# A hybrid decoder trunk in fp32 on one core: three norms without GpSimd, ten early pairs instead of seven, results ahead of other steps

## The chip, the cores and the metric

The kernel runs on one core of a Trainium2 chip. The metric is device time in microseconds of one execution; lower is better. The core has a matrix engine (PE in the profile), VectorE (DVE), ScalarE (ACT), GpSimd (POOL) and SyncE (SP), which here only starts DMAs. Each engine works through its own queue strictly in the order in which the instructions stand there, and waits for the others by semaphores. Matmul results lie in PSUM and are taken out by DVE or ACT.

## The reference

Two layers over a sequence of 1024 tokens with 1024 channels. Each layer has a token mixer and a SwiGLU FFN, both behind an RMS norm that is scaled and shifted by the conditioning.

```python
for l in range(DEPTH):
    mod = (c_act @ ada_w[l] + ada_b[l])[:, None, :]
    sh_m, sc_m, gt_m, sh_f, sc_f, gt_f = jnp.split(mod, 6, axis=-1)
    h = rms_norm(x, norm_mix[l]) * (1 + sc_m) + sh_m
    ...
        y = hybrid_mixer(h, ...)
    ...
        y = retention_mixer(h, ret_w_in[i], ret_w_out[i])
    x = x + gt_m * y
    h = rms_norm(x, norm_ffn[l]) * (1 + sc_f) + sh_f
    x = x + gt_f * swiglu(h, ffn_w_in[l], ffn_w_out[l])
```

`swiglu` is `(silu(g) * u) @ w_out` with `g, u` the halves of `h @ w_in` (2816 channels each). The retention's input product gives queries and keys, values and gates.

## The kernel before

**Layout and precision.** Activations lie transposed, channels on the 128 partitions: x is eight tiles x0 to x7 of 128 x 1024 tokens, and most work is done on a half of 512 tokens. Each fp32 operand v is split into a rounded part hi (a cast on ACT) and a remainder lo = v - hi (a subtraction on DVE or POOL), and a product takes three matmuls: hi hi, lo hi, hi lo (`mm3`, L161 to L163). Weights come by DMA as `raw` (512 KB), `w_split` makes `whi` (L141, ACT) and `wlo` (L142, DVE).

**Three large products with a norm ahead of them**: the FFN of layer 0, the retention's input product, the FFN of layer 1. Each stands behind an out product (`out_gen`) that runs one token half after the other; an output tile's eviction (L309, DVE) adds it to x. Two PSUM tiles take turns there, so that a group of 12 matmuls waits for the eviction two groups earlier. When the first half of x is done, `norm_ops` makes the norm of that half while the out product's second half still runs; the second half's norm follows.

**The norm.** `norm_stat` (L188) squares the eight tiles on ACT and adds them up: POOL takes five of the seven additions, DVE the two last. A matmul with a constant matrix (`nps`, L201) sums over the channels, `rsqrt` (L170 to L177) makes the root on ACT and DVE. `value` (L1210, L1211) makes a normed tile, `parts` (L1214, L1215) its hi and lo; every second lo of A11, A12 and A22 is on POOL, and a string ENGS says which engine makes the rest.

**The product.** The three products (of the retention all but the values) use a Strassen-Winograd scheme with seven block products instead of eight. A11, A12 are the first token half (upper and lower channels), A21, A22 the second; S1 to S4 are sums of these (L1251 to L1254, four steps each), split again into hi and lo (128 x 1024 each, `split`). B11 to B22 are blocks of a pair of weight tiles, T1 to T4 sums of them, made and split in `prep_b` (L1320 to L1328). `wino` runs over pairs. For a pair n: m1 multiplies A11 B11 and copies the result to u2 (L1350, ACT); m2 adds A12 B21 in the same PSUM bank, after that copy; m67 takes S2 T2 and S3 T3 (L1382, L1384), m5 S1 T1 (c22, L1391), m4 A22 T4, m3 S4 B22 in the bank of m5, after c22's addition has read it, and end (L1402) finishes u3. A block product has 12 matmuls (L1338 to L1340).

**Early pairs.** Only m1 and m2 need the first token half alone. In the FFNs they run ahead for the first NE = 7 pairs (`early`), with their results u2 and sg spilled to DRAM (`spill`) and read back in the main loop (`reload`); the weights of such a pair are loaded twice. sg has one buffer. Pair n's m2 follows its m1; the second half's norm is carried on after m1 of pair 1. The retention has no early pairs: its values (`v_rows`, L1771, evacuated by L1774 on ACT into two stage tiles) are multiplied on the first half meanwhile, three heads of four weight tiles each.

**What sets the order.** A scheduler places instructions of all engines by their dependences, its own estimates of duration, and a priority that `tc.high_priority(offset=...)` raises. The evictions L309 and the norm have 3000.

Of the kernel before, what the change touches and what calls it, by code (L numbers as in the profile page):

```python
# [13 lines left out]
ALU = mybir.AluOpType  # L14
# [4 lines left out]
D = 1024  # L19
# [14 lines left out]
GW = {'X': 1.4, 'W': 1.0, 'Y': 1.4, 'r': 1.0, 'v': 1.0, 'S': 1.2}  # L34
GSTAG = 14
EVP = 3000
NE = 7
ENGS = 'VGVGGGVVGGVGVVV'
EBS = 'VVVVVVVVV'
ECS = 'VVVVVVVGVVVVVVVVV'  # L40
RC = (2, 4)
# [21 lines left out]
def tile_trunk(ctx: ExitStack, tc: tile.TileContext, xT, cT, adaS, adaT, vec, w_ab, w_hyb, w_hout, w_rin, w_rout,  # L63
# [123 lines left out]
    def norm_stat(xs, scr, half):  # L187

        sl = slice(half * HT, half * HT + HT)
        acc = scr(1)  # L190
        for k in range(8):
            if k == 0:
                A.activation(acc, xs[k][:, sl], AF.Square)
            else:
                sq = scr(2 + k % 2)
                A.activation(sq, xs[k][:, sl], AF.Square)
                (V if k > 5 else G).tensor_tensor(acc, acc, sq, op=ALU.add)

        def rest():
            ps = pst.tile([P, HT], F32, tag="st", name="nps")  # L200
            PE.matmul(ps, onesD, acc, start=True, stop=True)  # L201
            y = scr(0)
            rsqrt(ps, y, acc)
            return y
        return rest
# [988 lines left out]
    def norm_ops(o, xs, pool, ni, kept, a21=None):  # L1194

        l, f = ni // 2, ni % 2
        half = int(bool(kept))
        sl = slice(half * HT, half * HT + HT)
        ts = {}

        def scr(i):
            if i == 0:
                return pool.tile([P, HT], F32, tag="ny", name="ny")
            j, r = divmod(i - 1, 2)
            if j not in ts:
                ts[j] = slot(12 + j, F32, "nscr")
            return ts[j][:, r * HT:r * HT + HT]

        def value(k, y, dst):
            V.scalar_tensor_tensor(dst, xs[k][:, sl], modA[:, ni * 8 + k:ni * 8 + k + 1], y, op0=ALU.mult, op1=ALU.mult)  # L1210
            A.activation(dst, dst, AF.Identity, bias=mcol(l, 3 * f, k))  # L1211

        def parts(hi, lo, v, eng):
            A.copy(hi, v)  # L1214
            eng.tensor_tensor(lo, v, hi.bitcast(F32), op=ALU.subtract)  # L1215

        part = lambda v, k: v[k // 2][:, (k % 2) * HT:(k % 2) * HT + HT]
        with tc.high_priority(offset=3000):
            rest = norm_stat(xs, scr, half)
        yield  # L1220
        with tc.high_priority(offset=3000):
            y = rest()
        if half == 0:
            kept["S3"] = [slot(14 + j, F32, "h11") for j in range(2)]
            kept["S4"] = [slot(22 + j, F32, "h12") for j in range(2)]
            for j in range(8):
                k, nm, v = j % 4, ("A11", "A12")[j // 4], part(kept[("S3", "S4")[j // 4]], j % 4)
                value(j, y, v)
                with tc.high_priority(offset=3000 if j < 4 else 0):
                    parts(o.get(nm, 0)[k], o.get(nm, 1)[k], v, G if k % 2 else V)  # L1230
            return
        v3, v4 = kept["S3"], kept["S4"]
        v1 = [slot(18 + j, F32, "h22") for j in range(2)]
        for k in range(4):
            value(4 + k, y, part(v1, k))
            parts(o.get("A22", 0)[k], o.get("A22", 1)[k], part(v1, k), G if k % 2 else V)
            yield
        v2 = [slot(i, F32, "S2v") for i in ((10, 11) if a21 else (8, 24))]

        def split(nm, j, v, hi, lo, eng):  # L1240
            if nm not in o.t:
                o.place(nm, {}, {})
            o.t[nm][0][j], o.t[nm][1][j] = hi, lo
            parts(o.tile(nm, 0, j), o.tile(nm, 1, j), v[j], eng)

        for k in range(4):
            h21 = pool.tile([P, HT], F32, tag="nh", name="nh", bufs=NNH)
            value(k, y, h21)
            if a21:
                parts(part(a21[0], k), part(a21[1], k), h21, V)  # L1250
            V.tensor_tensor(part(v3, k), part(v3, k), h21, op=ALU.subtract)  # L1251
            V.tensor_tensor(part(v2, k), part(v1, k), part(v3, k), op=ALU.subtract)
            ENG[0 if a21 else 8].tensor_tensor(part(v1, k), part(v1, k), h21, op=ALU.add)
            V.tensor_tensor(part(v4, k), part(v4, k), part(v2, k), op=ALU.subtract)  # L1254
            if not a21 and k % 2:
                split("S2", k // 2, v2, (9, 11)[k // 2], (10, 8)[k // 2], V)
            yield
        e = iter(ENG[1:8] if a21 else ENG[9:15])
        split("S3", 0, v3, 12, 24, next(e))
        yield  # L1260
        split("S3", 1, v3, 13, 14, next(e))
        yield
        if not a21:
            split("S1", 0, v1, 16, 15, next(e))
            split("S1", 1, v1, 17, 18, next(e))
            yield
            split("S4", 0, v4, 20, 19, next(e))
            split("S4", 1, v4, 21, 22, next(e))
            yield
            return  # L1270
        split("S4", 0, v4, 20, 15, next(e))
        yield
        split("S4", 1, v4, 21, 22, next(e))
        yield
        split("S2", 0, v2, 8, 9, G)
        split("S2", 1, v2, 10, 23, next(e))
        split("S1", 0, v1, 16, 11, next(e))
        split("S1", 1, v1, 17, 18, next(e))

    def wino(name, ops_of, fpa, npairs, ne, ev_of, step=lambda n, nm, w: None):  # L1280

# [7 lines left out]
        st = {}  # L1289
# [11 lines left out]
        def prep_e(n):  # L1301
            u = w_next()
            pairs[n] = dict(zip(("B11", "B21"), zip(*((t[:, 0:HT], t[:, HT:]) for t in u))))
# [43 lines left out]
        def m1(n):  # L1347
            s = st[n] = dict(A=bank("mA"), u2=tile_a("u2"))
            prod(n, s["A"], "A11", pairs[n]["B11"], True)
            A.copy(s["u2"], s["A"])  # L1350

        def m2(n):
            s = st[n]
# [21 lines left out]
        def m67(n, flip=False):  # L1375
            s = st[n]
            s["u3"] = tile_b("u3")
            for nm, w in (("S3", "T3"), ("S2", "T2")) if flip else (("S2", "T2"), ("S3", "T3")):
                s[nm] = bank("mB")
                prod(n, s[nm], nm, pairs[n][w], True)  # L1380
                if nm == "S2":
                    V.tensor_tensor(s["u2"], s["u2"], s["S2"], op=ALU.add)  # L1382
                if (nm == "S3") != flip:
                    V.tensor_tensor(s["u3"], s["u2"], s["S3"], op=ALU.add)  # L1384

        def m5(n):
            s = st[n]
            s["D"] = pg.tile([P, HT], F32, tag="g", name="mD")
            prod(n, s["D"], "S1", pairs[n]["T1"], True)
            s["c22"] = tile_b("c22")  # L1390
            V.tensor_tensor(s["c22"], s["u3"], s["D"], op=ALU.add)  # L1391
            ev_of(n).c22(n, s)

        def m3(n):
            s = st[n]
            prod(n, s["D"], "S4", pairs[n]["B22"], False)
            V.tensor_tensor(s["u2"], s["u2"], s["D"], op=ALU.add)
            ev_of(n).c12(n, s)

        def end(n):  # L1400
            s = st[n]
            V.tensor_tensor(s["u3"], s["u3"], s["E"], op=ALU.add)  # L1402
            ev_of(n).c21(n, s)

        def early(norm):
            banks()
            for n in range(ne):
                prep_e(n)
                m1(n)
                spill(n, 0, st[n]["u2"])  # L1410
                if n == 1:
                    for _ in range(5):
                        next(norm)
                m2(n)
                spill(n, 1, st[n]["sg"])
            prep_b(0)
            for _ in norm:
                pass
            reload(0)
# [340 lines left out]
    def v_rows(h, half, hi, lo, stage):  # L1760

        pss = [pv.tile([P, HT], F32, tag="v", name="rvps") for _ in range(4)]
        for j in range(4):
            whi, wlo = (t.rearrange("p (k c) -> p k c", k=2) for t in w_next())
            for tt in range(4):
                tk = slice(tt * P, tt * P + P)
                for i in range(2):
                    k = 2 * j + i
                    xh, xl = hi[k][:, tk], lo[k][:, tk]
                    for n, (a, b) in enumerate(((xh, whi), (xl, whi), (xh, wlo))):  # L1770
                        PE.matmul(pss[tt], a, b[:, i, :], start=(k + n == 0), stop=(k + n == 9))  # L1771
                if j == 3:
                    t = stage()
                    A.copy(t, pss[tt])  # L1774
                    nc.sync.dma_start(rv_d[h][:, half * 4 + tt, :], t)
            yield

# [347 lines left out]
```

## Time and profile before

| what | us |
|---|---|
| three runs | 3038.3, 3040.5, 3043.89 |
| median | 3040.5 |
| the profiled execution's own time | 3040.34 |
| its span, first to last instruction | 3038.6 |
| stage of the FFN norm, layer 0, and what follows | 839 to 1003 |
| stage of the retention's norm and its first half | 1504 to 1716 |
| stage of the FFN norm, layer 1, and what follows | 2351 to 2515 |

In the profile a row of the stage view gives start and end, length, then for each engine its busy time and number of instructions, then the clock granted to PE, the share of the DMA engines and their rate. A group row ends with busy time and mean duration, and with the idle time of its engine ahead of it. In the order of time, a bracket holds the engine's idle time ahead of a row and what ended it. `x`, `h`, `u` or `mA` are tile names; numbers are left out.

### The profile page before, as it was taken

Reading aid. Unit: us, or ns where it says so; the run is one execution under the profiler, and the core shown is the slowest. Engines: PE = TensorE matmul, PEld = TensorE weight load, DVE = VectorE, ACT = ScalarE, POOL = GpSimd, SP = SyncE. Lnnn points to the kernel's source line nnn. Section 1 sums busy time; section 2 is a strip of 40 time slices with the busy share of each in tenths; the row PEclk is TensorE's granted clock in tenths of the full one; section 3 lists DMA queues with packets and bytes.
Section 4 is the critical chain, followed back from the end, with each engine's and each line's share of the span. In section 5 each row is a group of like instructions: output and inputs, shape, how many; then the busy total and the mean of one; then the engine's idle time right before and its main releaser. Section 6 shows DMA issues by size and latency. Waiting matters only on the chain.

```text
span 3038.6 us, 41660 instructions
## 1 busy us (share of the span) xinstructions
PE 2939.2 (97%) x15640; PEld 2347.6 (77%) x15640; DVE 2214.9 (73%) x3353; ACT 1301.9 (43%) x2195; POOL 526.3 (17%) x526
## 2 busy tenths in 40 slices
PE   8999999999989999999989999999999899999999
PEld 4777787867767888877778788887777678888777
DVE  6677766699789887577772677578866987775775
ACT  5444455688663333233453333333233643332231
POOL 1222221276431111000120000001111311110000
PEclk9999999999999999999999999999999999999999
DMA  6333333331146545355454556362212564344543
GB/s 226 131 119 112 127 100 101 109 124 37 42 170 228 189 167 197 107 204 193 141 175 148 173 193 216 111 236 101 104 50 76 186 192 151 131 162 153 204 167 132
DMA packets 159866, 446.75 MB, mean 147 GB/s; under 512 B 19760, under 2 KB 28720, under 8 KB 159152
## 3 DMA queue, kind: packets, MB, share of 16 engines
q1 hardware_dynamic: 144976, 396.95, 38.3%
q0 software_dynamic: 14224, 46.35, 4.1%
q8 instruction: 123, 2.02, 0.3%
q10 hardware_dynamic: 464, 0.79, 0.1%
q14 instruction: 79, 0.65, 0.1%
HBM read 325.00 MB, written 119.01 MB: 146 GB/s over the span
## 4 chain that ended last, share of the span: by engine, by line
PE 72%; DVE 16%; DMA 5%; issue 3%; ACT 2%; POOL 1%; SPq 0%; DVEq 0%; ACTq 0%; POOLq 0%
PE rvps L1771 4%; PE mD L1339 4%; PE mD L1340 4%; PE mD L1338 4%; PE mA L1338 4%; PE mA L1339 4%; PE mA L1340 4%; PE mB L1340 4%; PE mB L1339 4%; PE mB L1338 4%; PE ops L161 3%; PE ops L162 3%; PE ops L163 3%; PE gps L161 3%; PE gps L163 2%
## 5 line engine op out<-in xcount | busy, mean ns | idle before, releaser
L142 DVE TENSOR_TENSOR wlo<-raw,whi 128x1024 fp32r<-128x1024 f32 x124 | 162.8, 1314 | 98.2 <-ACT whi L141 94.3
L141 ACT CAST whi<-raw 128x1024 fp32r<-128x1024 f32 x126 | 131.9, 1049 | 195.1 <-PE ops L162 85.1
L309 DVE SCALAR_TENSOR_TENSOR x<-ops,mod,x 128x512 f32<-128x512 f32 x160 | 119.5, 747 | 106.7 <-PE ops L163 106.2
L1319 ACT CAST whi<-raw 128x512 fp32r<-128x512 f32 x152 | 88.5, 620 | 224.2 <-PE mA L1339 192.2
L1319 ACT CAST thi<-raw 128x512 fp32r<-128x512 f32 x228 | 129.5, 619 | 109.8 <-DVE raw L1325 81.6
L161 PE MATMUL gps<-hh,whi 128*128 128x512 f32 x352 | 166.1, 472 | 0.0
L1320 DVE TENSOR_TENSOR tlo<-raw,thi 128x512 fp32r<-128x512 f32 x228 | 150.2, 704 | 2.8 <-ACT thi L1319 2.8
L1012 POOL TENSOR_TENSOR sl<-ab,sh 128x512 fp32r<-128x512 f32 (+1 forms) x80 | 116.4, 1455 | 149.9 <-ACT ab L996 82.9
L163 PE MATMUL gps<-hh,wlo 128*128 128x512 f32 x352 | 139.9, 398 | 0.0
L162 PE MATMUL gps<-hl,whi 128*128 128x512 f32 x352 | 139.5, 396 | 0.0
L161 PE MATMUL ops<-osh,whi 128*128 128x512 f32 x320 | 128.4, 406 | 10.2 <-DVE x L309 8.1
L1320 DVE TENSOR_TENSOR wlo<-raw,whi 128x512 fp32r<-128x512 f32 x152 | 98.9, 686 | 53.6 <-ACT whi L1319 53.6
L1297 ACT CAST whi<-raw 128x1024 fp32r<-128x1024 f32 x62 | 65.2, 1051 | 167.1 <-DMA raw<-in_w_fin_dram 61.3
L162 PE MATMUL ops<-osl,whi 128*128 128x512 f32 x320 | 127.9, 401 | 4.9 <-DVE osl L1976 4.3
L1338 PE MATMUL mA<-A12h,whi 128*128 128x512 f32 x304 | 120.5, 396 | 7.4 <-ACT u L1350 7.4
L1298 DVE TENSOR_TENSOR wlo<-raw,whi 128x1024 fp32r<-128x1024 f32 x62 | 77.2, 1246 | 68.7 <-ACT whi L1297 68.6
L1338 PE MATMUL mD<-S4h,whi 128*128 128x512 f32 x304 | 119.5, 393 | 7.3 <-DVE c L1391 7.3
L163 PE MATMUL ops<-osh,wlo 128*128 128x512 f32 x320 | 126.4, 396 | 0.0
L1339 PE MATMUL mD<-S1l,whi 128*128 128x512 f32 x304 | 118.8, 391 | 6.5 <-DVE S1l L1552 6.5
L1513 POOL DMA_DIRECT2D hop_d<-x x128 | 69.1, 541 | 314.0 <-ACT x L1510 203.8
L1486 ACT ACTIVATE u<-u 128x512 f32<-128x512 f32 x44 | 27.8, 633 | 221.1 <-DVE u L1402 221.1
L1340 PE MATMUL mA<-A11h,wlo 128*128 128x512 f32 x304 | 119.4, 394 | 2.1 <-DVE wlo L142 2.1
(459 smaller groups left out, 9065.9 us busy)
## 6 DMA issues: line engine op xcount, KB each, us to landing
raw<-in_w_fin_dram SPq DMA_DIRECT2D x102, 512.0 KB, 4.2
hop_d<-x POOLq DMA_DIRECT2D x176, 256.0 KB, 3.8
raw<-in_w_rin_dram SPq DMA_DIRECT2D x64, 512.0 KB, 4.3
raw<-in_w_fout_dram SPq DMA_DIRECT2D x52, 512.0 KB, 4.4
gth<-in_adaT_dram SPq DMA_DIRECT2D x64, 256.0 KB, 2.9
x<-in_adaT_dram SPq DMA_DIRECT2D x32, 512.0 KB, 5.3
raw<-in_w_hyb_dram SPq DMA_DIRECT2D x28, 512.0 KB, 3.8
x_d<-x SPq DMA_DIRECT2D x24, 512.0 KB, 3.1
```

The lines of the kernel that those rows point to most:

```text
L141: A.copy(hi, raw)
L142: eng.tensor_tensor(lo, raw, hi.bitcast(F32), op=ALU.subtract)
L161: PE.matmul(ps, whi, xh, start=start, stop=False)
L162: PE.matmul(ps, whi, xl, start=False, stop=False)
L163: PE.matmul(ps, wlo, xh, start=False, stop=stop)
L309: V.scalar_tensor_tensor(xs[dt][:, sl], ps, gts(dt), xs[dt][:, sl], op0=ALU.mult, op1=ALU.add)
L1319: A.copy(hi, t)
L1320: e.tensor_tensor(lo, t, f32(hi), op=ALU.subtract)
L1338: PE.matmul(ps, w[0][:, c], xh[k], start=(start and k == 0), stop=False, skip_group_check=True)
L1339: PE.matmul(ps, w[0][:, c], xl[k], start=False, stop=False, skip_group_check=True)
L1340: PE.matmul(ps, w[1][:, c], xh[k], start=False, stop=(k == 3), skip_group_check=True)
L1771: PE.matmul(pss[tt], a, b[:, i, :], start=(k + n == 0), stop=(k + n == 9))
```

## The change

1. `norm_stat`, `parts` of A11, A12 and A22, and all of ENGS: DVE in place of POOL (four of the L1253 additions and the halves of S1, S3 and S4 among them).
2. The second half's sum of squares loses its high priority; in the first half `value` of A11 gets it too, `value` of A12 keeps none.
3. NE is 10. m2 of pair 0 waits until m1 of pair 1 stands; the weights of pairs 0 and 1 are split at priority 2000.
4. `EV`, priority 3000, for the instructions that take m1, m67, m5, m3 and end out of PSUM, and for the evacuation in `v_rows`.

```diff
-NE = 7
-ENGS = 'VGVGGGVVGGVGVVV'
+NE = 10
+ENGS = 'VVVVVVVVVVVVVVV'
...
-                (V if k > 5 else G).tensor_tensor(acc, acc, sq, op=ALU.add)
+                V.tensor_tensor(acc, acc, sq, op=ALU.add)
...
-        with tc.high_priority(offset=3000):
+        with tc.high_priority(offset=0 if half else 3000):
             rest = norm_stat(xs, scr, half)
...
-                value(j, y, v)
                 with tc.high_priority(offset=3000 if j < 4 else 0):
-                    parts(o.get(nm, 0)[k], o.get(nm, 1)[k], v, G if k % 2 else V)
+                    value(j, y, v)
+                    parts(o.get(nm, 0)[k], o.get(nm, 1)[k], v, V)
...
-            parts(o.get("A22", 0)[k], o.get("A22", 1)[k], part(v1, k), G if k % 2 else V)
+            parts(o.get("A22", 0)[k], o.get("A22", 1)[k], part(v1, k), V)
...
-        split("S2", 0, v2, 8, 9, G)
+        split("S2", 0, v2, 8, 9, V)
...
+    EV = lambda: tc.high_priority(offset=3000)
...
-            A.copy(s["u2"], s["A"])
+            with EV():
+                A.copy(s["u2"], s["A"])
...
-            V.tensor_tensor(s["c22"], s["u3"], s["D"], op=ALU.add)
+            with EV():
+                V.tensor_tensor(s["c22"], s["u3"], s["D"], op=ALU.add)
...
-                prep_e(n)
+                with tc.high_priority(offset=2000 if n < 2 else 0):
+                    prep_e(n)
                 m1(n)
...
-                m2(n)
-                spill(n, 1, st[n]["sg"])
+                for i in ((), (0, 1), (n,))[min(n, 2)]:
+                    m2(i)
+                    spill(i, 1, st[i]["sg"])
...
-                    A.copy(t, pss[tt])
+                    with EV():
+                        A.copy(t, pss[tt])
```

The EV blocks around u2 and u3 in m67, m3 and end read the same way.

What this does to the queues is shown at two places. The first is DVE in the retention, from the last evictions of the out product (L309) to the root of the second half (L175 to L177); L1215 are remainders, L142 remainders of weights for `v_rows`, L197 additions of squares. Before:

```order
L309 SCALAR_TENSOR_TENSOR x_6323<-ops,mod,x_6323 128x512
L1215 TENSOR_TENSOR A12l<-h_13755,A12h 128x512
L197 TENSOR_TENSOR nscr<-nscr 128x512
L309 SCALAR_TENSOR_TENSOR x_6324<-ops,mod,x_6324 128x512
L142 TENSOR_TENSOR wlo<-raw,whi 128x1024
L197 TENSOR_TENSOR nscr<-nscr 128x512
L142 TENSOR_TENSOR wlo<-raw,whi 128x1024
L175 SCALAR_TENSOR_TENSOR nscr<-nps,nscr 128x512
L176 TENSOR_SCALAR nscr<-nscr 128x512
L177 TENSOR_TENSOR ny<-ny,nscr 128x512
L142 TENSOR_TENSOR wlo<-raw,whi 128x1024
```

With the change:

```order
L309 SCALAR_TENSOR_TENSOR x_6324<-ops,mod,x_6324 128x512
L142 TENSOR_TENSOR wlo<-raw,whi 128x1024 x2
L197 TENSOR_TENSOR nscr<-nscr 128x512 x5
L142 TENSOR_TENSOR wlo<-raw,whi 128x1024
L197 TENSOR_TENSOR nscr<-nscr 128x512 x2
L142 TENSOR_TENSOR wlo<-raw,whi 128x1024
L175 SCALAR_TENSOR_TENSOR nscr<-nps,nscr 128x512
L176 TENSOR_SCALAR nscr<-nscr 128x512
L142 TENSOR_TENSOR wlo<-raw,whi 128x1024
L177 TENSOR_TENSOR ny<-ny,nscr 128x512
```

All seven additions of squares now stand on DVE behind the last eviction, and four weight remainders, in place of two, stand ahead of the root's first step. Both FFNs have the same rows here. Behind this, the next weight remainder stands 28 instructions on; before, two of them lay among those steps.

The second place is ACT at the retention's first pair. L1774 (L1784 with the change) is the evacuation of `v_rows`, `thi` the hi of T2, T3 and T4, `whi` that of a weight (L1297, L1299 in `prep_a`), and `u` the copy of m1. Before:

```order
L1774 COPY rvt<-rvps 128x512
L1319 CAST thi_14989<-raw 128x512
L1774 COPY rvt<-rvps 128x512
L1319 CAST thi_14991<-raw 128x512
L1319 CAST thi_14995<-raw 128x512
L1774 COPY rvt<-rvps 128x512 x2
L1297 CAST whi<-raw 128x1024
L1350 COPY u_15047<-mA 128x512
```

With the change:

```order
L1784 COPY rvt<-rvps 128x512 x2
L1321 CAST thi_15016<-raw 128x512
L1321 CAST thi_15018<-raw 128x512
L1321 CAST thi_15022<-raw 128x512
L1784 COPY rvt<-rvps 128x512 x2
L1353 COPY u_15074<-mA 128x512
L1299 CAST whi<-raw 128x1024
```

The second evacuation moved ahead of all three casts of T, and the copy of m1 ahead of the cast of the next weight.

More of the change, by code (lines that the diff above doesn't have):

```diff
@@ L1380, in m67 @@
                 prod(n, s[nm], nm, pairs[n][w], True)
[L1381 to L1384, printed above, removed]
+                with EV():
+                    if nm == "S2":
+                        V.tensor_tensor(s["u2"], s["u2"], s["S2"], op=ALU.add)
+                    if (nm == "S3") != flip:
+                        V.tensor_tensor(s["u3"], s["u2"], s["S3"], op=ALU.add)
         def m5(n):
@@ L1396, in m3 @@
             prod(n, s["D"], "S4", pairs[n]["B22"], False)
-            V.tensor_tensor(s["u2"], s["u2"], s["D"], op=ALU.add)
+            with EV():
+                V.tensor_tensor(s["u2"], s["u2"], s["D"], op=ALU.add)
             ev_of(n).c12(n, s)
@@ L1401, in end @@
             s = st[n]
-            V.tensor_tensor(s["u3"], s["u3"], s["E"], op=ALU.add)
+            with EV():
+                V.tensor_tensor(s["u3"], s["u3"], s["E"], op=ALU.add)
             ev_of(n).c21(n, s)
@@ L1773, in v_rows @@
                     t = stage()
-                    A.copy(t, pss[tt])
+                    with EV():
+                        A.copy(t, pss[tt])
                     nc.sync.dma_start(rv_d[h][:, half * 4 + tt, :], t)
```

## The prediction

> **What bounds the kernel now.** I read the page's engine shares first.
>
> ```profile
> span 3038.6 us, 41660 instructions
> PE 2939.2 (97%) x15640; PEld 2347.6 (77%) x15640; DVE 2214.9 (73%) x3353; ACT 1301.9 (43%) x2195; POOL 526.3 (17%) x526
> ```
>
> PE is busy 97% of the span, and the change adds or removes no matmul. It can only win time in which PE stands still or runs slowly around the three norms that it touches. So the next view is the busy time by stage, with stages cut at these norms: the FFN of layer 0 (from 839), the retention (from 1504) and the FFN of layer 1 (from 2351).
>
> ```profile
> core 0: us, PE busy (x) PEld busy (x) DVE busy (x) ACT busy (x) POOL busy (x), PEclk, DMA share, GB/s
> 839.00:866.00 27.00, 23.08 (x90) 17.42 (x89) 23.13 (x25) 18.51 (x29) 14.26 (x9) 0.94 0.51 186
> 866.00:907.00 41.00, 36.59 (x156) 28.42 (x154) 37.73 (x41) 28.84 (x43) 13.12 (x7) 1.00 0.53 179
> 907.00:934.60 27.60, 24.53 (x99) 19.12 (x98) 24.20 (x36) 11.52 (x22) 3.93 (x3) 0.94 0.57 186
> 934.60:1003.00 68.40, 67.04 (x295) 54.86 (x294) 64.31 (x114) 26.86 (x49) 14.26 (x27) 1.00 0.71 234
> 1504.00:1531.00 27.00, 23.08 (x91) 17.46 (x90) 23.18 (x26) 18.51 (x29) 14.47 (x9) 0.94 0.47 175
> 1531.00:1566.00 35.00, 31.02 (x131) 23.86 (x130) 32.76 (x42) 22.05 (x32) 6.88 (x3) 1.00 0.57 197
> 1566.00:1688.00 122.00, 122.00 (x540) 101.02 (x539) 38.04 (x30) 41.93 (x53) 11.84 (x4) 1.00 0.46 147
> 1688.00:1716.00 28.00, 24.75 (x107) 19.52 (x106) 20.86 (x33) 9.11 (x18) 0.00 (x0) 1.00 0.66 229
> 2351.00:2378.00 27.00, 23.07 (x90) 17.44 (x89) 23.14 (x25) 18.51 (x29) 14.26 (x9) 0.94 0.47 176
> 2378.00:2420.00 42.00, 38.11 (x151) 29.73 (x150) 38.42 (x42) 29.81 (x44) 13.05 (x7) 0.92 0.58 194
> 2420.00:2447.00 27.00, 25.29 (x112) 20.46 (x111) 22.38 (x31) 10.94 (x18) 3.90 (x3) 1.00 0.57 175
> 2447.00:2515.00 68.00, 66.63 (x293) 54.43 (x292) 60.38 (x98) 25.73 (x44) 14.48 (x27) 1.00 0.64 205
> ```
>
> The row 1566:1688 is PE without a wait: 122.00 / 540 = 0.226 us a matmul. Length minus matmuls times 0.226 is what a stage loses, slow matmuls included: 6.7, 5.8, 5.2 and 1.8 in the FFN of layer 0; 6.4, 5.4 and 3.8 in the retention; 6.7, 7.9, 1.7 and 1.8 in the FFN of layer 1. Together 53 us, 1.7% of the span: a ceiling. PE's waits over the same stages name whom it waits for (microseconds, times, longest): first layer 0, then the retention, then layer 1.
>
> ```profile
> PE ops L161 <- DVE x L309: 3.9, 3, 2.2
> PE mD L1338 <- DVE c L1391: 3.6, 3, 2.3
> PE mA L1338 <- ACT u L1350: 3.4, 2, 2.4
> ...
> PE rvps L1771 <- ACT rvt L1774: 2.4, 2, 1.5
> PE rvps L1771 <- DVE wlo L142: 1.5, 1, 1.5
> PE mA L1338 <- ACT rvt L1774: 1.4, 1, 1.4
> ...
> PE mA L1338 <- ACT u L1350: 2.8, 1, 2.8
> ```
>
> The first row stands in all three stages: the out product waits for its own evictions, which DVE does late. Why DVE is late is seen where DVE and POOL run side by side.
>
> ```profile
> 846.19 4.16 DVE L1210 SCALAR_TENSOR_TENSOR h<-x,modA,ny 128x512 f32<-128x512 f32 x3
> 846.35 3.44 POOL L197 TENSOR_TENSOR nscr<-nscr 128x512 f32<-128x512 f32 x2 [12.33 <-ACT nscr L193]
> 1560.59 0.68 DVE L1251 TENSOR_TENSOR h<-h,nh 128x512 f32<-128x512 f32 x1
> 1561.19 0.68 DVE L1253 TENSOR_TENSOR h<-h,nh 128x512 f32<-128x512 f32 x1
> L1210 DVE SCALAR_TENSOR_TENSOR nh<-x,modA,ny 128x512 f32<-128x512 f32 x4 | 6.1, 1537 | 0.0
> L1210 DVE SCALAR_TENSOR_TENSOR h<-x,modA,ny 128x512 f32<-128x512 f32 x4 | 2.7, 746 | 0.0
> ```
>
> Alone such an instruction takes 746 ns. Beside two POOL additions three took 4.16 us, some 2 us too long: a POOL addition of 1.7 us costs DVE about 1 us, while DVE itself would need 0.60 us for it (1561.19 - 1560.59, start to start).
>
> **The change, part by part.** The sum is made against the profiled execution, 3040.34 us (span 3038.6 and 1.7 around it), which is the median of the runs, 3040.5, within 0.01%.
>
> *Evictions of the second half (three times 27 us).* Here POOL is busy 14.3 us; that work goes: five squares' additions are now behind the eviction of x7, four remainders (A11l, A12l) are on DVE. Between the evictions of x0 and x7 DVE then has 8 evictions and 8 values at 0.66 us, 8 remainders at 0.60, the root's three (1.7) and one weight remainder (1.2): 18.3 us, against seven groups of 12 matmuls, 19.0 us of PE. DVE keeps up. Left is the two-pass matmul of the first sum, 0.7, and 0.2 of a late start: 6.7, 6.4, 6.7 become 0.9 each. Gain 17.1. If DVE falls one eviction behind it is some 1 us less a time; below zero would need POOL to help, which the 4.16 us row excludes.
>
> That gain has a slow tail in it: after a wait of over 2 us PE runs slowly for a while.
>
> ```profile
> 860.72 0.50 PE L161 MATMUL ops<-osh,whi 128*128 128x512 f32 x1 [2.23 <-DVE x L309]
> ...
> 861.28 0.59 PE L163 MATMUL ops<-osh,wlo 128*128 128x512 f32 x1
> 861.67 0.63 PE L161 MATMUL ops<-osh,whi 128*128 128x512 f32 x1
> ```
>
> The granted clock of 0.94 over these 27 us is 1.6 us of it; the stages at 0.94 and 0.92 later hold 1.7 and 3.4: 9.9 in all five. The Trainium skill ("TensorE: Matmul & The Clock Gate", Part 1: The HAM clock gate) puts the drop after an idle window of some 3.4 us. These rows show it after 2.23, so by that rule the tails would not hang on these waits; it is a rival below.
>
> *First product on the first half, two FFNs (5.8 and 7.9 lost).* The wait for the first weight's remainder stays (1.2 on DVE, still behind the eviction of x7), as does the sum's matmul (0.7). The waits for u2 (3.4 with what follows it, 2.8 and its tail 3.4) came from an evacuation that stood on ACT behind casts of 1.05; now it stands ahead of them, but a cast that has begun is not stopped, so I leave 0.9. Left 2.7 each: gain 3.1 + 5.2. All the wait gone would be 1.8 more; none gone, 6.5 less.
>
> *Second half's operands.* The second sum is now at low priority: its matmul stands 38 instead of 7 matmuls into the product, 7.0 us later. DVE's rows at the eviction of x7 and at the first T2 remainder:
>
> ```profile
> 865.36 0.75 DVE L309 SCALAR_TENSOR_TENSOR x<-ops,mod,x 128x512 f32<-128x512 f32 x1 [1.39 <-PE ops L163]
> 908.21 3.48 DVE L1320 TENSOR_TENSOR tlo<-raw,thi 128x512 fp32r<-128x512 f32 x2
> ```
>
> That is 42.9 us. Now: +7.0; minus POOL's delays, 13.1 us of POOL (866:907) at 1 us in 1.7, 7.7; plus on DVE two A22 remainders and four additions (3.6), five more halves of S1, S3 and S4 ahead of it (5.7), a weight remainder and a step (1.8): 53.3. PE has three pairs more: 2.0 + 225 x 0.226 + 0.7 = 53.6 before it needs that T2. So DVE just holds; the margin is 0.3 us and what PE loses on the way. I take no wait.
>
> *First pair of the main loop (5.2 and 1.7).* The wait for c22 in layer 0 came from prep_b of the next pair, eight instructions on DVE that began late:
>
> ```profile
> 919.01 0.69 DVE L1322 TENSOR_TENSOR raw<-raw 128x512 f32<-128x512 f32 x1 [1.51 <-DMA raw<-in_w_fin_dram]
> ```
>
> Those weights were late since POOL had held up DVE's last T remainders (the 3.48 above, for two). With POOL gone they are asked for 3 us earlier relative to S2. Left 1.0 each: gain 4.2 + 0.7. The other waits for c22 stay: in the new order it stands behind the same seven instructions of prep_b. Three more pairs run in the short cycle (60 matmuls beside a reload), which loses 0.3 a pair (1.8 / 6): 0.9 worse in each FFN, -1.8. Their three extra weight loads, spills and reloads lie on SP's queue beside a DMA share of 0.5 to 0.7.
>
> *Retention, first half (5.4 lost).* Here no pair is added, so the later sum bites. DVE at the eviction of x7 and at the sixth weight remainder:
>
> ```profile
> 1530.89 0.75 DVE L309 SCALAR_TENSOR_TENSOR x<-ops,mod,x 128x512 f32<-128x512 f32 x1 [1.16 <-PE ops L163]
> 1563.60 1.21 DVE L142 TENSOR_TENSOR wlo<-raw,whi 128x1024 fp32r<-128x1024 f32 x1
> ```
>
> It started 32.7 us after x7, and PE, its waits for rvt (2.4) and for it (1.5) taken out, had wanted it at 30.0. Now: +7.0 for the sum; minus POOL's delays (6.9 us of POOL, 4.0); plus 1.2 for two A22 remainders; minus 2.3, as two weight remainders are done earlier; plus 0.5 to 2.2 for DVE's waits for ACT, which holds the v evacuations ahead of casts. Start 35.1 to 36.8, ready 1.2 later. PE takes four more hi products first and wants it at 30.9: a wait of 5.4 to 7.1 and a slow tail of 1.6, while the waits for rvt go. With the sum's matmul 0.7, left 7.7 to 9.4; I take 9.0, near the upper end, because of ACT's order: loss 3.6. Lower end: none of the wait, a gain of 3; upper end: another 2 lost.
>
> *Retention, first pair (3.8 lost).* The v evacuations now precede the casts of T (wait 1.4 gone) and u2 precedes a cast that waited for its weights:
>
> ```profile
> 1697.05 1.05 ACT L1297 CAST whi<-raw 128x1024 fp32r<-128x1024 f32 x1 [3.56 <-DMA raw<-in_w_rin_dram]
> 1698.00 0.58 ACT L1350 COPY u<-mA 128x512 f32<-128x512 f32 x1
> ```
>
> Left 1.0 for c22: gain 2.8 (0 if the store of v, which frees the stage, is what ends last; 3.6 at most).
>
> The other results at high priority (u3, c22 and so on in later pairs) cost nothing: PE shows no wait for them there.
>
> Sum: 17.1 + 8.3 + 4.9 - 1.8 - 3.6 + 2.8 = 27.7 us; 3040.3 - 27.7 = **3012.6 us**.
>
> **Rivals.**
> 1. *DVE becomes the bound of both FFNs' first S2.* For it: a margin of 0.3 us, and DVE waits for ACT that I left out. Against: PE loses some too. 5 us late and a tail of 1.6, twice, and 2 more in the retention: 3027.8.
> 2. *The slow tails stay*, tied to the clock's own window and not to the wait. Against: every stage without a wait over 2 us shows 1.00. 9.9 less gained: 3022.5. That is what the skill's 3.4 us would make of it.
> 3. *The change doesn't do what it says*: the evictions are late for DVE's own load, and its remainders replace the delays. 17.1 not gained: 3029.7. Against: the 746 and 1537 above.
> 4. *More is gained*: no wait in the retention (5.4 becomes 2.2, 6.8 better) and no wait for u2 (1.8): 3004.0.
> 5. *Slower: the spills set the pace.* sg has one buffer, and its copy waits until the spill before has landed; u2 stands behind it on ACT.
>
> ```profile
> 2400.70 5.37 DMA early_d<-sg
> early_d<-sg SPq DMA_DIRECT2D x5, 256.0 KB, 2.1
> ```
>
> A pair has 24 matmuls, 5.4 us; copy, issue and landing make L + 1.0. Over 20 pairs that eats the 27.7 from L = 5.8. At 6.5, a little over the 5.37 that one spill took, it is 42 us: 3054. Against: the median is 2.1.
>
> **How the numbers follow.** Forecast 0.52 (its own range 3006 to 3020), rival 1 0.17, rival 2 0.05, rival 3 0.06, rival 4 0.15, rival 5 0.05. The range leaves out rival 5, the upper part of 1 and 3 and the lowest of 4: 3001 to 3031. A measurement of this kernel tells some 0.2% (6 us) from no change, so faster means below 3034.4: forecast, rivals 2 and 4 and most of 1 and 3, 0.90; within, 0.05; slower, rival 5, 0.05.
>
> **What would show it.** In the new profile: DVE's L1210 at 0.75 everywhere and no wait of ops for x around the second half's evictions (else rival 3); granted clock 1.00 there (else 2); the first S2 product without a wait over 1 us (else 1); one wait of 5 us or more of rvps for a weight remainder some 31 us into the retention's first half (else 4); spills that land in under 3 us (else 5). A prediction off by more than 15 us means that DVE's or ACT's queue stalls at a place that I took from the order alone.

## The result and the profile after

The changed kernel takes 3009.89 us (median of 4 runs, 3007.9 to 3013.84) against 3039.4 us (median of 4 runs of the kernel before, beside it): a ratio of 0.990, 95% interval 0.989 to 0.991, so it is 1% faster. The profiled execution took 3011.29 us. First the page of the changed kernel, engine shares:

```profile
span 3009.3 us, 41663 instructions
PE 2927.6 (97%) x15640; PEld 2342.6 (78%) x15640; DVE 2208.4 (73%) x3418; ACT 1305.8 (43%) x2201; POOL 414.2 (14%) x461
```

POOL lost 112 us of work, but DVE, which took it over, is busy 6.5 us less than before: what POOL did had cost DVE more than doing it itself. PE's busy time fell by 11.6 us with the same matmuls, so part of the gain is slow matmuls that became fast ones.

The next view is the changed kernel's retention, cut at the same numbers of matmuls as before, with the same columns (length, busy time and instructions of each engine, granted clock, DMA share, rate):

```profile
1489.30:1510.10 20.80, 20.80 (x91) 16.58 (x90) 18.12 (x29) 16.15 (x25) 0.00 (x0) 1.00 0.60 225
1510.10:1548.10 38.00, 30.86 (x130) 24.08 (x129) 33.48 (x49) 24.27 (x36) 0.00 (x0) 0.97 0.55 181
1548.10:1672.30 124.20, 124.20 (x540) 102.55 (x539) 41.65 (x40) 43.08 (x56) 0.00 (x0) 0.98 0.45 144
1672.30:1699.30 27.00, 24.60 (x107) 19.47 (x106) 18.11 (x31) 8.45 (x17) 0.00 (x0) 1.00 0.72 243
```

In the FFNs such cuts would mislead: three more pairs now stand ahead of the first S2, so that the same number of matmuls is no longer the same work. There both kernels are cut at the first S2 matmul, at the end of the first pair's m3 and at the end of the product. Layer 0, before and then with the change:

```profile
839.50:907.80 68.30, 59.55 (x243) 45.57 (x241) 61.16 (x66) 47.97 (x74) 27.38 (x16) 0.98 0.52 181
907.80:928.60 20.80, 18.15 (x72) 14.25 (x73) 18.98 (x28) 8.23 (x15) 2.78 (x1) 0.94 0.52 164
928.60:1456.80 528.20, 523.16 (x2293) 429.71 (x2292) 401.69 (x637) 182.22 (x307) 47.50 (x88) 1.00 0.53 184
838.00:912.60 74.60, 73.30 (x316) 58.18 (x314) 68.32 (x94) 56.25 (x85) 0.00 (x0) 1.00 0.61 208
912.60:929.00 16.40, 16.40 (x73) 13.44 (x72) 10.57 (x20) 6.99 (x13) 0.00 (x0) 1.00 0.60 196
929.00:1442.10 513.10, 506.79 (x2222) 415.57 (x2221) 397.55 (x635) 178.07 (x302) 47.52 (x88) 1.00 0.55 193
```

Layer 1:

```profile
2351.50:2421.20 69.70, 61.88 (x243) 47.86 (x242) 62.25 (x68) 49.10 (x74) 28.17 (x17) 0.93 0.52 184
2421.20:2439.60 18.40, 16.69 (x73) 13.36 (x72) 15.26 (x20) 7.24 (x11) 1.92 (x1) 1.00 0.51 148
2439.60:2967.40 527.80, 522.47 (x2293) 429.26 (x2293) 387.33 (x575) 177.72 (x277) 47.44 (x88) 1.00 0.47 168
2336.60:2411.50 74.90, 73.43 (x316) 58.16 (x315) 67.86 (x92) 56.07 (x84) 0.00 (x0) 1.00 0.61 215
2411.50:2427.90 16.40, 16.40 (x74) 13.45 (x73) 9.63 (x16) 6.76 (x11) 0.00 (x0) 1.00 0.56 179
2427.90:2938.80 510.90, 505.85 (x2221) 415.72 (x2220) 381.40 (x571) 173.06 (x271) 47.47 (x88) 1.00 0.50 176
```

Length minus matmuls times 0.226 is again what a stage loses. Counted by their starts, the three stages of an FFN hold 242, 72 and 2292 matmuls before and 314, 72 and 2220 with the change. The forecast column holds the prediction's terms, put together for these stages.

| stage | lost before | lost after | gained | forecast gain |
|---|---|---|---|---|
| FFN layer 0: up to the first S2 | 13.6 | 3.6 | 10.0 | 8.9 |
| first pair of the main loop | 4.5 | 0.1 | 4.4 | 4.2 |
| later pairs | 10.2 | 11.4 | -1.2 | -0.9 |
| retention: evictions | 6.4 | 0.2 | 6.2 | 5.5 |
| first half (38.0 and 124.2 together) | 5.4 | 10.8 | -5.4 | -3.6 |
| first pair | 3.8 | 2.8 | 1.0 | 2.8 |
| FFN layer 1: up to the first S2 | 15.0 | 3.9 | 11.1 | 11.0 |
| first pair of the main loop | 2.1 | 0.1 | 2.0 | 0.7 |
| later pairs | 9.8 | 9.2 | 0.6 | -0.9 |
| sum | 70.8 | 42.1 | 28.7 | 27.7 |

The stages gain 28.7 us where 27.7 were forecast, and the execution as a whole 29.05 (3040.34 - 3011.29). A single trace does not settle differences of a microsecond or two: the part ahead of 839, which the edits hardly touch, came out between 1.0 us slower and 2.7 us quicker than before in the eleven traces taken since.

PE's waits in the changed kernel (us, times, longest), first layer 0 up to 987 and then the retention:

```profile
PE mA L1342 <- DVE wlo L142: 1.3, 1, 1.3
PE mD L1340 <- DVE c L1396: 0.9, 1, 0.9
...
PE rvps L1780 <- DVE wlo L142: 6.3, 2, 5.9
PE mD L1340 <- DVE c L1396: 1.8, 1, 1.8
PE rvps L1780 <- ACT rvt L1784: 0.9, 1, 0.9
PE mA L1340 <- ACT rvt L1784: 0.6, 1, 0.6
```

The waits of `ops` for x and of `mA` for u2 are gone. One large wait is new, in the retention. DVE's rows there, and PE's behind it:

```profile
1510.04 0.75 DVE L309 SCALAR_TENSOR_TENSOR x<-ops,mod,x 128x512 f32<-128x512 f32 x1 [0.17 <-PE ops L163]
1546.28 1.22 DVE L142 TENSOR_TENSOR wlo<-raw,whi 128x1024 fp32r<-128x1024 f32 x1
1547.56 0.80 PE L1780 MATMUL rvps<-wlo,A11h 128*128 128x512 f32 x1 [5.89 <-DVE wlo L142]
1548.15 0.63 PE L1780 MATMUL rvps<-whi,A11h 128*128 128x512 f32 x1
```

The sixth weight remainder starts 36.2 us after x7's eviction. PE waits 5.89 us for it, and then runs slowly: the rows of 0.63 us go on to 1552.

### The profile page after: what moved, and what is told of

It reads as the page before. It is cut to its first block, busy times and chain, and to the rows that moved or that the text cites. A ratio compares the mean times of both kernels' runs of the same rounds, so it can differ in the third digit from the quotient of the medians.

```text
span 3009.3 us, 41663 instructions
## 1 busy us (share of the span) xinstructions
PE 2927.6 (97%) x15640; PEld 2342.6 (78%) x15640; DVE 2208.4 (73%) x3418; ACT 1305.8 (43%) x2201; POOL 414.2 (14%) x461
## 4 chain that ended last, share of the span: by engine, by line
PE 77%; DVE 12%; DMA 5%; issue 3%; ACT 2%; POOL 1%; SPq 0%; DVEq 0%; ACTq 0%; POOLq 0%
PE rvps L1780 4%; PE mA L1340 4%; PE mA L1342 4%; PE mA L1341 4%; PE mD L1341 4%; PE mD L1340 4%; PE mD L1342 4%; PE ops L161 4%; PE mB L1342 4%; PE mB L1341 4%; PE mB L1340 4%; PE ops L162 4%; PE ops L163 4%; PE gps L161 3%; PE gps L162 2%
## 5 line engine op out<-in xcount | busy, mean ns | idle before, releaser
L142 DVE TENSOR_TENSOR wlo<-raw,whi 128x1024 fp32r<-128x1024 f32 x130 | 164.6, 1268 | 98.2 <-ACT whi L141 95.6
L309 DVE SCALAR_TENSOR_TENSOR x<-ops,mod,x 128x512 f32<-128x512 f32 x160 | 119.7, 749 | 89.5 <-PE ops L163 89.0
L1910 POOL TENSOR_TENSOR qd<-kq,tab 128x512 f32<-128x512 f32 x16 | 28.3, 1787 | 966.2 <-DVE kq L1858 819.2
L1299 ACT CAST whi<-raw 128x1024 fp32r<-128x1024 f32 x56 | 58.9, 1052 | 153.0 <-DMA raw<-in_w_rin_dram 50.2
L1342 PE MATMUL mA<-A12h,wlo 128*128 128x512 f32 x304 | 119.2, 392 | 0.0
```

The lines of the kernel that those rows point to most:

```text
L142: eng.tensor_tensor(lo, raw, hi.bitcast(F32), op=ALU.subtract)
L309: V.scalar_tensor_tensor(xs[dt][:, sl], ps, gts(dt), xs[dt][:, sl], op0=ALU.mult, op1=ALU.add)
L1342: PE.matmul(ps, w[1][:, c], xh[k], start=False, stop=(k == 3), skip_group_check=True)
```

## Experiments

Each of the ten is set against the kernel before, measured beside it on the same chip.

**Part 1 undone.**

```diff
-ENGS = 'VVVVVVVVVVVVVVV'
+ENGS = 'VGVGGGVVGGVGVVV'
...
-                V.tensor_tensor(acc, acc, sq, op=ALU.add)
+                (V if k > 5 else G).tensor_tensor(acc, acc, sq, op=ALU.add)
```

The remainders of A11, A12 and A22 and the first half of S2 go back to POOL in the same way.

> The changed kernel with part 1 undone: the squares' additions, every second remainder of A11, A12 and A22, and the steps of ENGS are on POOL again; the later second sum, ten pairs and the priorities stay. My theory (a POOL addition of 1.7 us costs DVE about 1 us, and POOL takes three times as long for the same addition): in the second half of the out product four remainders on POOL cost DVE some 4 us and save it 2.4, so the evictions are about 1 us late a site, 3 us; the five squares' additions on POOL put the second root some 5 us later, which the first S2 of both FFNs, with a margin of about 1 us in the profile of the changed kernel, must show as a wait of some 5 us with a slow tail of 2, 14 us in all: about 3027, with DVE's L1210 again at 1.1 us or more in the mean. Rival (DVE's own load made the evictions late and POOL costs it nothing): DVE has less to do than with the change, no wait comes back, 3008 to 3012.

Measured: 3045.83 us, ratio 1.002 (1.001 to 1.003): slower than before the change. PE's waits behind the evictions in layer 0, with part 1 undone:

```profile
PE mA L1340 <- ACT u L1353: 5.5, 3, 4.2
PE nps L201 <- DVE nscr L197: 4.2, 1, 4.2
```

The rival, by which no wait comes back, falls. But most of the loss is not what POOL costs DVE: L1210 is at 1179 ns again in the eviction stage of layer 0, yet that stage loses only 2.3 us (22.60 us for 90 matmuls). The wait of 4.2 us comes from POOL's own slower chain: three of its late additions take 4.77 us, and DVE stands idle 1.86 us for the last of them. What POOL costs DVE by itself is settled by the run after the next. The size was wrong too, 36 us instead of 17: I had looked for the late sum at the first S2, while it is the sum's own matmul that holds PE for 4.2 us, at all three places, with slow matmuls behind it, and the copies of u2 fall behind as well (4.2 us at most). The late sum of part 2 works only when DVE does the adding.

**Part 1 alone.** The kernel before, with exactly the edits that the last kernel undid, and nothing else.

> The kernel before with part 1 alone: all that work moves from POOL to DVE, the second sum keeps its high priority, seven pairs, no new priorities. My theory: the three stages of the evictions gain most of their 17 us, less about 1 a site, as DVE now adds the squares between the evictions too (22.9 us of work against 19.0, of which A12's part can stand back); the first pair's wait for c22 in layer 0 goes as well (about 4); the waits for u2 stay. About 3022, within 3018 to 3027, granted clock 1.00 over the evictions. Rival (the evictions are late for DVE's own load): 4.6 us more on DVE in each of these stages makes the wait for x longer, 3040 to 3050.

Measured: 3018.11 us, ratio 0.993 (0.992 to 0.994). The three eviction stages, cut at the same matmuls:

```profile
839.40:861.50 22.10, 20.32 (x89) 16.31 (x87) 19.53 (x32) 18.04 (x27) 0.00 (x0) 1.00 0.65 244
1497.50:1518.30 20.80, 20.80 (x91) 16.67 (x91) 18.19 (x29) 16.36 (x25) 0.00 (x0) 1.00 0.58 218
2336.10:2358.30 22.20, 20.40 (x90) 16.34 (x88) 19.62 (x32) 18.04 (x27) 0.00 (x0) 1.00 0.61 233
```

27.0 us became 22.1, 20.8 and 22.2, at a clock of 1.00. DVE has more to do between the evictions and is no longer late for them. Some 22 of the 30 us are part 1's. The waits for u2 are gone here as well (0 in layer 0, 0.8 us in layer 1), without any of the priorities that I had credited. New are waits of 1.8 us for the sum and 1.9 us for the first weight's remainder in each FFN.

**POOL's additions put back as idle work.** The changed kernel, plus five additions a site that nobody needs:

```diff
+        if half:
+            with tc.high_priority(offset=3000):
+                for k in range(5):
+                    G.tensor_tensor(scr(4), xs[k][:, sl], xs[k][:, sl], op=ALU.add)
         with tc.high_priority(offset=0 if half else 3000):
             rest = norm_stat(xs, scr, half)
```

> The changed kernel plus five POOL additions a site, of an evicted half tile of x0 to x4 to itself, into scratch that nobody reads, each free to start when its tile is evicted; DVE's order is the same, and nothing waits for POOL. This measures what POOL costs DVE by itself. My theory: an addition of 1.7 us costs DVE about 1 us, 5 us a site. DVE has 18.3 us of work beside 19.0 of PE there, so the evictions come some 4 us late in the sum of a site, with slow matmuls after waits over 2 us: 4 to 7 us a site, 3022 to 3031. Rival (POOL and DVE run side by side without cost, and the earlier gain came from the shorter chain of the sum): 3008 to 3012, all L1210 and L309 at 0.75.

Measured: 3016.11 us, ratio 0.992 (0.990 to 0.993), against 0.990 (0.989 to 0.991) for the changed kernel; these intervals touch, so the trace decides. One place of it in layer 0, POOL's row and then DVE's:

```profile
848.18 1.41 POOL L1221 TENSOR_TENSOR nscr<-x 128x512 f32<-128x512 f32 x1 [2.49 <-DVE x L309]
...
847.96 3.51 DVE L1210 SCALAR_TENSOR_TENSOR h<-x,modA,ny 128x512 f32<-128x512 f32 x4
```

And its group of L1210 on DVE in that stage (busy time, mean ns):

```profile
L1210 DVE SCALAR_TENSOR_TENSOR h<-x,modA,ny 128x512 f32<-128x512 f32 x8 | 7.3, 949 | 0.0
```

Four L1210 take 3.51 us beside the addition, 2.74 without one (in the last experiment's trace). Over each of the three stages the kernel loses 2.2 to 2.3 us against the changed one at the same matmuls. So POOL's work costs DVE time although nothing waits for POOL: the rival falls. The price is about 0.5 us an addition here (2.3 / 5) and not 1: these read one tile and took 1.26 us in the mean, the first fell into idle time of DVE, and the last ran mostly beside an eviction, which is not slowed. The three between them cost some 0.8 us each (3.51 for 2.74 here).

**Seven pairs.**

```diff
-NE = 10
+NE = 7
```

> The changed kernel with NE = 7 in place of 10. My theory: the three pairs are the cover for the second half's operands. In the profile of the changed kernel the first remainder of T2 starts 53.3 and 53.6 us after x7's eviction, and PE reads it 1 to 2 us later; with seven pairs PE is there 72 matmuls, 16.3 us, sooner, DVE only some 3.4 us (three weight remainders) plus what the order moves behind. A wait of 5 to 10 us before the first S2 in both FFNs, each with a slow tail of 2 to 3, less 1.8 for three pairs that run in the long cycle: 3022 to 3033. Rival (the pairs are not needed, since DVE without POOL's delays is in time anyway): 3006 to 3010, no wait over 1 us at the first S2.

Measured: 3027.81 us, ratio 0.996 (0.995 to 0.997), in the expected range. PE's waits in layer 1 from the first S2 on:

```profile
PE mD L1340 <- DVE c L1396: 4.1, 3, 1.6
PE mB L1340 <- ACT thi L1321: 4.0, 4, 2.4
PE mB L1342 <- DVE tlo L1322: 0.7, 2, 0.4
```

The price is right, its form is not: no single wait of 5 to 10 us, but several smaller ones over the first pairs of the main loop, as the order interleaves the T steps with the late norm. Nearly all of it is paid in layer 1: cut like the table above, that FFN loses 27.7 us instead of 13.2, and the one of layer 0 only 17.8 instead of 15.1.

**The sum early again at all three places, with ten pairs.**

```diff
-        with tc.high_priority(offset=0 if half else 3000):
+        with tc.high_priority(offset=3000):
             rest = norm_stat(xs, scr, half)
```

> The changed kernel with the second half's sum at priority 3000 at all three places. My theory: in the retention it gains 5 to 7 as when it is early there alone; in the FFNs the ten pairs cover the late sum, so nothing is gained, and the squares' additions between the evictions cost 2 to 3 in each (the kernel before with part 1 alone shows waits of 1.8 for the sum and 1.9 for the first weight's remainder in each FFN): 3006 to 3011. Rival (the late sum costs the FFNs too): 3000 or less.

Measured: 3018.27 us, ratio 0.993 (0.992 to 0.994): a miss by 7 us. PE's waits over the evictions in layer 0 (layer 1 has 2.6 and 1.6):

```profile
PE nps L201 <- DVE nscr L197: 2.6, 1, 2.6
PE mA L1342 <- DVE wlo L142: 1.8, 1, 1.8
```

With two waits so close, slow matmuls follow, and each FFN loses 5 to 7 us; the retention gains some 5. Four kernels now make a square:

| | seven pairs | ten pairs |
|---|---|---|
| sum early | 3018.1 | 3018.3 |
| sum late | 3027.8 | 3009.9 |

(The first one also lacks the priorities and the order of pairs 0 and 1; the next two runs show that EV and that order gain nothing in the changed kernel.) Neither edit gains alone: the late sum clears the evictions, and the three pairs cover the later operands.

**No EV.**

```diff
-    EV = lambda: tc.high_priority(offset=3000)
+    EV = lambda: tc.high_priority(offset=0)
```

> The changed kernel without the EV priority (offset 0 in EV), all else as in it. My theory: the copies of u2 and the evacuations of the values stand behind casts again. Waits for u2 in the first product of both FFNs, 3 us each with what follows them, in layer 1 with a slow tail, 6.5 in all; in the retention's first pair 2 to 3 more: about 3019, within 3014 to 3023. Rival (the order of A11 and A12 and the earlier weights of pairs 0 and 1 took the waits for u2 away, EV does nothing): 3008 to 3012.

Measured: 3010.39 us, ratio 0.990 (0.989 to 0.992). My theory falls: one wait for u2 of 0.7 us in layer 0, none in layer 1. In the retention the wait for the sixth remainder is 3.5 instead of 5.9 us, and the waits for rvt 2.1 instead of 1.5: EV moved the loss and took none away that can be measured.

**The order of pairs 0 and 1 undone.**

```diff
-                with tc.high_priority(offset=2000 if n < 2 else 0):
+                with tc.high_priority(offset=0):
                     prep_e(n)
...
-                for i in ((), (0, 1), (n,))[min(n, 2)]:
-                    m2(i)
-                    spill(i, 1, st[i]["sg"])
+                m2(n)
+                spill(n, 1, st[n]["sg"])
```

> The changed kernel with m2 straight behind m1 in pairs 0 and 1 and their weights split at normal priority, EV kept. The waits for u2 went, and without EV they stay away. Theory after that run: they went with POOL, since the kernel before with part 1 alone and the old order shows 0 and 0.8 us of them. Then this kernel loses nothing but a shorter cover for the copies of pairs 0 and 1: 3009 to 3013. Rival (the order of pairs 0 and 1 and their early weights took the waits away): waits for u2 of 3 us a FFN and more come back, 3016 or more.

Measured: 3010.64 us, ratio 0.991 (0.990 to 0.993); no wait for u2. This part does nothing that can be measured either.

**Every spill of sg written twice.**

```diff
             nc.sync.dma_start(early_d[2 * n + i], t)
+            if i == 1:
+                nc.sync.dma_start(early_x[n], t)
```

> The changed kernel with every spill of sg written a second time, to another place in DRAM: ten more DMAs of 256 KB on SP's queue in each FFN, and sg comes free only when both have landed. My theory: the spills of sg land in 2.0 to 2.2 us in the median against a break-even of 5.8, so sg still comes free within a pair's 5.4 us: 3008 to 3014. Rival (the spills are near the point where they set the pace, through the copy of sg that holds up the copy of u2 behind it on ACT): a second landing of 2 to 3 us shows as waits for u2 of 1 us or more in several pairs, 3016 to 3040.

Measured: 3013.04 us, ratio 0.991 (0.989 to 0.993). Its DMA groups in layer 0 (count, size, median us from issue to landing):

```profile
early_d<-sg SPq DMA_DIRECT2D x10, 256.0 KB, 2.1
early_x<-sg SPq DMA_DIRECT2D x10, 256.0 KB, 2.5
```

The longest wait for u2 is 0.6 us. Rival 5 falls with room to spare.

**The sum early in the retention alone.**

```diff
-        with tc.high_priority(offset=0 if half else 3000):
+        with tc.high_priority(offset=0 if half and not a21 else 3000):
             rest = norm_stat(xs, scr, half)
```

> The changed kernel with the second half's sum of squares at priority 3000 again in the retention alone. My theory: the later sum is what puts the sixth weight remainder 36.2 us behind x7's eviction, and so makes the one wait of 5.9 us there with its slow tail of about 2.7. With the sum early again and POOL still out of it the wait goes; against that the squares' additions stand between the evictions once more and cost about 1 to 3 us there (the kernel before with part 1 alone shows 1.9 for the remainder and 0.9 for the sum in the retention). Gain 5 to 7: about 3004. Rival (the wait comes from ACT's new order or from the work that POOL no longer does, not from the sum): the wait stays above 3 us, 3008 to 3012.

Measured: 3006.93 us, ratio 0.989 (0.988 to 0.991). The wait of 5.9 us is gone; waits of 1.7 us for the sum and 1.8 us for a weight remainder come in its place. By the traces the retention's stages are 5 us better than in the changed kernel; the medians differ by 3, which the intervals do not tell apart.

**The value weights' splits first.**

```diff
     steps = 0
+    wpri[0] = 3000
     for h in range(3):
...
+    wpri[0] = 0
     rp = RetParts()
```

> The changed kernel with the splits of the value weights at priority 3000 while the retention's first half runs; the sum stays late. My theory: the wait is one of place in DVE's queue alone; the sixth remainder moves ahead of some twenty norm steps, the norm's steps have room behind it, and the wait of 5.9 us and its tail of 2.7 go: about 3001, within 2999 to 3004. Rival (DVE is full there, so that the wait only moves to the seventh or eighth remainder or to the second half's operands): 3007 to 3011.

Measured: 3000.38 us (2997.76 to 3005.53), ratio 0.9875 (0.986 to 0.989): the fastest kernel of this study. DVE's rows of x7's eviction and of the sixth remainder:

```profile
1508.93 0.75 DVE L309 SCALAR_TENSOR_TENSOR x<-ops,mod,x 128x512 f32<-128x512 f32 x1 [0.17 <-PE ops L163]
...
1528.00 1.21 DVE L142 TENSOR_TENSOR wlo<-raw,whi 128x1024 fp32r<-128x1024 f32 x1
```

The stages of the retention's first half and first pair:

```profile
1509.00:1539.90 30.90, 30.45 (x131) 23.97 (x130) 27.42 (x37) 20.94 (x32) 0.00 (x0) 1.00 0.71 240
1539.90:1661.80 121.90, 121.90 (x539) 100.95 (x538) 47.44 (x50) 46.07 (x61) 0.00 (x0) 1.00 0.45 143
1661.80:1687.50 25.70, 24.56 (x107) 19.48 (x106) 18.14 (x31) 8.58 (x17) 0.00 (x0) 1.00 0.74 256
```

19.1 instead of 36.2 us after x7, and the three stages lose 1.3, 0.1 and 1.5 us instead of 10.8 (two stages) and 2.8. DVE was not short of time there; its queue had the wrong row first. The sum can stay late.

## Why the prediction was right, and where it was not

3012.6 was forecast and 3009.9 measured, inside the forecast's own range. The main step, the evictions, held for its stated reason; several smaller ones did not, and their errors cancel in good part. The steps:

- **Evictions: right, and for the stated reason.** Part 1 alone gives most of it, POOL's idle work takes part of it back, and L1210 is back at its short duration. Its group over layer 0's stage, before and with the change, rules out rival 3:

```profile
L1210 DVE SCALAR_TENSOR_TENSOR h<-x,modA,ny 128x512 f32<-128x512 f32 x8 | 10.8, 1389 | 0.0
L1210 DVE SCALAR_TENSOR_TENSOR h<-x,modA,ny 128x512 f32<-128x512 f32 x8 | 5.7, 753 | 0.0
```

- **Slow tails: right.** They went with the waits, the stages without a wait over 2 us show a clock of 1.00, and rival 2 is dead. Not every wait over 2 us brings a tail, though (last section).
- **First product of the FFNs: right in size, wrong in cause.** I laid the waits for u2 to ACT's casts and their end to EV. Without EV they stay away, and with part 1 alone they go. On ACT in the kernel before, the rows that I should have read stand some way ahead of the copy of u2. In layer 0:

```profile
898.28 1.05 ACT L1214 CAST S3h<-h 128x1024 fp32r<-128x1024 f32 x1 [2.38 <-DVE h L1251]
...
902.35 0.58 ACT L1350 COPY u<-mA 128x512 f32<-128x512 f32 x1
```

  From 898.28 on ACT works almost without a pause. The copy does stand behind casts, but these were late because ACT had waited 2.38 us for DVE; there a weight remainder (L142) had just taken 2.32 us beside a POOL addition, where 1.22 is its usual time. That fits the end of the wait with part 1 alone; no run tests it by itself. In layer 1:

```profile
2406.17 0.59 ACT L1358 COPY sg<-mA 128x512 f32<-128x512 f32 x1 [1.72 <-DMA early_d<-sg]
...
2407.59 0.59 ACT L1350 COPY u<-mA 128x512 f32<-128x512 f32 x1
```

  ACT stood 1.72 us for the late landing of one spill. Whether that landing was late by chance or because of the order of that moment, no run here settles.
- **Second half's operands: right.** The changed kernel's first T2 remainder in layer 0 starts 53.3 us after x7's eviction (911.09 - 857.77), exactly as forecast; in layer 1 it is 53.6.

```profile
857.77 0.75 DVE L309 SCALAR_TENSOR_TENSOR x<-ops,mod,x 128x512 f32<-128x512 f32 x1 [0.17 <-PE ops L163]
911.09 0.69 DVE L1322 TENSOR_TENSOR tlo<-raw,thi 128x512 fp32r<-128x512 f32 x1
913.05 0.39 PE L1342 MATMUL mB<-S2h,tlo 128*128 128x512 f32 x1
```

  It is done at 911.78 and PE reads it at 913.05: a margin of 1.3 us where I had 0.3. Rival 1 did not happen, with some luck: the 0.3 set PE's time, 53.6, against the remainder's start and left out the 0.69 us that it takes, so by the sum's own figures DVE would have been late by 0.4; PE came only 55.3 us after the eviction. With seven pairs 18 us are lost, nearly all in layer 1.
- **First pair and later pairs of the FFNs: right for the first pair, uncertain for the later ones.** c22 of the first pair keeps no wait (0.1 us lost instead of 1.0 each): 6.4 us are gained where 4.9 were forecast. With part 1 alone it loses 0.7 and 0.1, so POOL's absence is enough for that, as stated. Behind it, with three more pairs in the short cycle, layer 0 loses 1.2 us more than before and layer 1 0.6 less, where 0.9 more was forecast for each: 0.6 in all instead of 1.8, too little for single traces to confirm the 0.3 a pair.
- **Retention's first half: right, a little small.** The start of 36.2 us lies within 35.1 to 36.8, the wait of 5.89 within 5.4 to 7.1. The slow tail was mis-sized: one matmul at 0.594, ten at 0.427 and one at 0.345 instead of 0.226 us are 2.5 us, not 1.6; 1.5 us of the waits for rvt are left, which were to go. Rival 4 has no wait here and is out.
- **Retention's first pair: mis-sized.** 2.8 us are left, not 1.0. The wait for c22 grew from 0.7 to 1.8 us, since DVE begins the pair only when the cast of its weights is done:

```profile
1682.94 1.23 DVE L1300 TENSOR_TENSOR wlo<-raw,whi 128x1024 fp32r<-128x1024 f32 x1 [4.96 <-ACT whi L1299]
```

  So the copy of u2 ahead of that cast helped PE reach c22 sooner and did not make c22 earlier.

Too little for the FFNs (26.9 gained instead of 23.0) and too much for the retention (1.8 instead of 4.7) cancel in good part: that the total came out so close is partly luck.

## What to carry to other kernels

Handing small work to an idle engine is not free where the engine beside it stalls for it: look for one instruction form with two durations, the longer one beside the other engine. When a step is moved to a later place, go through everything that is queued behind it on its engine and ask which row PE wants first; here one priority on the value weights' splits was worth another 9.5 us. Edits that come in one change may need each other (late sum and ten pairs) or do nothing (EV), which only undoing them one at a time shows.

## What the runs showed of the hardware

**POOL slows some DVE instructions and not others.** In the kernel before, over the whole trace (min, median, max in ns):

```profile
L309 DVE SCALAR_TENSOR_TENSOR x<-ops,mod,x x160: 736/750/753, 650.9 to 3034.1; 128x512 f32<-128x512 f32 x160
L1210 DVE SCALAR_TENSOR_TENSOR h<-x,modA,ny x36: 735/749/1795, 846.2 to 2388.1; 128x512 f32<-128x512 f32 x36
```

Both are the same operation of the same size. L1210 takes its tensors from SBUF and up to 1795 ns; L309, with one operand from PSUM, never takes more than 753, though 22 of its 160 ran with a POOL tensor operation beside them for over 70% of their time. The Trainium skill ("SBUF — State Buffer", SBUF: two separate sides) says that DVE with two SBUF inputs and GpSimd exclude each other for a whole instruction; these rows agree, the eviction being the case outside the rule.

**The slow tail has a threshold near 2 us, and it is not sharp.** These are the matmuls of 128x512 behind 830 us in all twelve traces, a wait being a matmul's time from start to start beyond 0.229 us. 56 waits of 0.9 to 1.98 us that stood alone had no slow matmul behind them; of 13 from 2.03 us up, nine were followed by 5 to 13 matmuls of 0.427 us, and four (2.08, 2.09, 2.34 and 3.19) were not. Nor was one of 2.56 in the kernel before, which had a shorter wait 26 matmuls ahead of it. Two waits close together did it too (1.7 and 1.8 us by the list of waits, with the sum early in the retention alone). The idle window of 3.4 us that the Trainium skill gives ("TensorE: Matmul & The Clock Gate", Part 1: The HAM clock gate) is too long for these waits; the measurement decides.
